# Chaining the score products and the value products of a sliding-window attention so that two head groups alternate on TensorE

## The chip, the cores and the metric

The kernel runs on one core of one Trainium2 chip. The metric is the device time of one execution in microseconds. Three runs of the kernel before gave 2683.91, 2685.73 and 2686.53 us; their median is 2685.73 us.

## What is computed

One decoder block over 2048 tokens of width 1024, in float32: an adaptive norm, one wide projection, two token mixers side by side (sliding-window attention with sinks, and a chunkwise mLSTM), their gated merge, and a SwiGLU feed-forward part. The change touches only the attention. Cut to that:

```python
# 8 query heads in 2 groups of 4, one key/value head of width 64 to each group
# blocks of 128 queries; each sees its own and the previous block of 128 keys
s = einsum('bnqhgd,bnkhd->bnhgqk', qb, kb)          # scores, 128 x 256 to a head
s = where(mask, s, -inf)
m = maximum(max(s), sink)
p = exp(s - m); p = p / (sum(p) + exp(sink - m))
o = einsum('bnhgqk,bnkhd->bnqhgd', p, vb)           # values with probabilities
```

## The kernel before

**Stages.** The sequence is worked in two superblocks of 1024 tokens. In each, the projection's big products (tiles `acc`, left operand `whi`/`wlo` or `big`, written as a high and a low part so that three float32r products make one of float32 accuracy) fill TensorE, and the attention and the mLSTM are woven between them as generators ("streams"). After both superblocks comes the feed-forward part, with no attention in it. The streams of superblock 0 that matter here run from 99 to 300 us of the profiled execution, those of superblock 1 from 774 to 977 us.

**One attention block** (`attention`, line 899) has 128 queries, n = 0 to 15. Two streams (`attention_stream`, line 980) take the even and the odd n. Its steps:

- Lines 915 to 931, twice (a half step each, `jj` = 0 and 1): two PSUM banks, one for each head group g, from a pool of four (`mix`). Twelve score products follow: two heads `u`, three products each (high with high, high with low, low with high), and for each of them g = 0 and g = 1. A product of g = 0 uses rows 0 to 63 of TensorE's array, one of g = 1 rows 64 to 127, because each head is 64 wide. ScalarE then copies the bank out (line 927) and VectorE merges the other half of the keys in (line 929).
- Lines 932 to 946: maximum, exponentials on ScalarE (line 942), sums, and a multiplication by the reciprocal on GpSimd (line 946).
- Lines 949 to 961: for each g, four transposes of the probabilities on TensorE (line 216), a copy on ScalarE (line 955, `pf`) and, for n > 0, a masked copy on VectorE (line 959, `pc`).
- Lines 962 to 965: four products of values with probabilities, `pf` of g = 0 and 1, then `pc` of g = 0 and 1 (two for n = 0). A product of g = 0 fills columns 0 to 63 of the array, one of g = 1 columns 64 to 127. Each shows as two matmul records in the trace.
- Lines 967 to 975: ScalarE casts the sum out (line 968) and issues DMAs for it and for the next block's operands (lines 970, 896, 975).

**What sets the order.** The generators fix the order in which instructions are traced. Before line 1576 each instruction is pinned to that order; after it a list scheduler orders each engine's instructions anew, by its own estimate of when operands are ready and buffers free. It keeps data dependencies and the few explicit order edges, nothing else, so products that are traced in turn need not stand in turn. `mm` (line 207) issues a matmul and returns nothing. [...]

In the profile all products of `mm` have line 211 and all transposes line 216: they are told apart by their tiles. `mix<-at` are scores, `mix<-tm,at` the products with values, `acc<-...` the projection.

## Time and profile before

| what | value |
|---|---|
| median of three runs | 2685.73 us |
| the profiled execution | 2687.54 us, of which the span is 2685.5 us |
| TensorE busy | 2629.6 us (98% of the span), 12382 matmul records |
| VectorE, ScalarE, GpSimd busy | 1988.3, 1298.8, 140.4 us |
| score products | 384, from 99.3 to 949.5 us |
| products with values | 62 (124 records), from 124.0 to 976.8 us |
| granted TensorE clock, mean | 0.993 |

How to read it: a row of the timeline gives the start, the time from the first start to the last end of the merged instructions, engine, line, operation, tiles, shapes and count; in brackets stand the idle time of that engine ahead of the row and what ended it. Matmuls overlap in the array, so what one costs is read from its start to the start of the next, not from its length.

### The profile page before, as it was taken

The numbers are of one execution on the slowest core, as the hardware profiler recorded it, in microseconds if no ns is written. First come the engines' busy times: TensorE is split into PE (matmuls) and PEld (weight loads), VectorE is DVE, ScalarE is ACT, GpSimd is POOL, SyncE is SP. The second block draws the span as 40 slices with busy tenths as digits, with TensorE's granted clock in tenths as the row PEclk, the third lists the DMA queues.
The fourth block names the chain that finished last, engine by engine and source line by source line (L and its number), as shares of the span: only waits on it lengthen the run. The fifth ranks groups of instructions, "written<-read, shape, count | busy, mean of one in ns | idle before, by whom it ended". The sixth has DMA issues, their size and how long they took to land.

```text
span 2685.5 us, 35800 instructions
## 1 busy us (share of the span) xinstructions
PE 2629.6 (98%) x12382; PEld 2146.8 (80%) x12382; DVE 1988.3 (74%) x3882; ACT 1298.8 (48%) x2525; POOL 140.4 (5%) x181
## 2 busy tenths in 40 slices
PE   7899999999998999999999999999999999999998
PEld 6777788888886778888877888888777888888886
DVE  7888887768696988876677777775677676666466
ACT  4656544545754654444654343335554333333444
POOL 0100001200101000110000000000000000000000
PEclk9999999999999999999999999999999999999999
DMA  7564456897575644678775555446675232334566
GB/s 252 173 231 144 148 175 185 263 345 246 191 245 160 210 141 151 194 239 321 227 243 176 181 180 180 134 143 219 214 247 188 98 114 97 108 99 148 189 204 219
DMA packets 353637, 511.89 MB, mean 191 GB/s; under 512 B 25120, under 2 KB 213660, under 8 KB 348208
## 3 DMA queue, kind: packets, MB, share of 16 engines
q1 hardware_dynamic: 335240, 493.82, 55.4%
q10 hardware_dynamic: 18216, 15.79, 2.0%
q8 instruction: 97, 1.59, 0.2%
q14 instruction: 84, 0.69, 0.1%
HBM read 357.12 MB, written 144.02 MB: 187 GB/s over the span
## 4 chain that ended last, share of the span: by engine, by line
PE 63%; DVE 3%; DMA 1%; ACT 1%; issue 0%; POOL 0%; SPq 0%; DVEq 0%; POOLq 0%; ACTq 0%
PE acc L211 42%; PE mix L211 20%; DVE hl L1608 1%; PE mix L216 1%; DMA raw<-as_d 1%; ACT hl L1607 1%; DMA raw<-ws_d 0%; DMA raw<-in_w_ffn_down_dram 0%; DVE big L1608 0%; DVE w L1918 0%; DVE big L1931 0%; DVE w L1954 0%; DVE w L1959 0%; ACT big L1653 0%; POOL rs L457 0%
## 5 line engine op out<-in xcount | busy, mean ns | idle before, releaser
L211 PE MATMUL acc<-big,hl 128*128 128x512 f32 x3936 | 933.9, 392 | 1.4 <-ACT hl L1607 0.7
L211 PEld LDWEIGHTS acc<-big,hl 128*128 128x128 f32 x3936 | 732.9, 188 | 164.8 <-issue 10.0
L1607 ACT CAST hl<-raw 128x512 fp32r<-128x512 f32 x732 | 440.7, 621 | 504.7 <-PE acc L211 238.7
L1608 DVE TENSOR_TENSOR hl<-raw,hl 128x512 fp32r<-128x512 f32 x732 | 497.5, 695 | 190.1 <-ACT hl L1607 187.8
L211 PE MATMUL acc<-whi,big 128*128 128x512 f32 (+1 forms) x1216 | 356.7, 374 | 7.9 <-ACT tx L89 3.8
L211 PE MATMUL mix<-big,hl 128*128 128x512 f32 x1056 | 263.0, 390 | 1.7 <-ACT hl L1607 1.0
L211 PEld LDWEIGHTS acc<-whi,big 128*128 128x128 f32 x1216 | 222.1, 191 | 50.9 <-ACT tx L89 4.3
L211 PE MATMUL acc<-hl,hl 128*128 128x512 f32 x1008 | 238.8, 395 | 5.8 <-DVE hl L1608 3.4
L211 PEld LDWEIGHTS mix<-big,hl 128*128 128x128 f32 x1056 | 197.7, 188 | 44.5 <-ACT hl L1607 1.9
L211 PEld LDWEIGHTS acc<-hl,hl 128*128 128x128 f32 x1008 | 188.0, 189 | 52.1 <-DVE hl L1608 8.4
L211 PE MATMUL acc<-wlo,big 128*128 128x512 f32 (+1 forms) x608 | 226.0, 374 | 3.0 <-DVE wlo L267 3.0
L211 PE MATMUL mix<-hl,hl 128*128 128x512 f32 x792 | 182.6, 391 | 1.1 <-DVE hl L1608 0.9
L211 PEld LDWEIGHTS mix<-hl,hl 128*128 128x128 f32 x792 | 147.9, 188 | 34.8 <-DVE hl L1608 3.0
L211 PE MATMUL acc<-big,whi 128*128 128x512 f32 x512 | 158.2, 393 | 0.0
L267 DVE TENSOR_TENSOR wlo<-raw,whi 128x1024 fp32r<-128x1024 f32 (+1 forms) x95 | 109.8, 1156 | 64.6 <-ACT whi L266 58.4
L266 ACT CAST whi<-raw 128x1024 fp32r<-128x1024 f32 (+1 forms) x95 | 93.7, 987 | 112.5 <-PE acc L211 102.5
L211 PEld LDWEIGHTS acc<-wlo,big 128*128 128x128 f32 x608 | 115.6, 190 | 24.0 <-DVE wlo L267 4.6
L457 POOL TENSOR_TENSOR rs<-ms,halves 128x1 f32<-128x1 f32 (+1 forms) x56 | 43.6, 791 | 1647.1 <-DVE ms L455 1637.5
L211 PE MATMUL mix<-hcT4h,hl 128*128 128x512 f32 x352 | 115.6, 389 | 0.7 <-ACT hl L1607 0.7
L211 PE MATMUL acc<-hcT2h,hl 128*128 128x512 f32 x352 | 115.5, 389 | 0.0
L211 PEld LDWEIGHTS acc<-big,whi 128*128 128x128 f32 x512 | 95.4, 188 | 19.6 <-DMA big<-y_d 0.4
L211 PE MATMUL acc<-big,wlo 128*128 128x512 f32 x256 | 97.6, 392 | 0.0
(350 smaller groups left out, 3537.2 us busy)
## 6 DMA issues: line engine op xcount, KB each, us to landing
raw<-in_w_in_dram SPq DMA_DIRECT2D x48, 1024.0 KB, 6.7
as_d<-w SPq DMA_DIRECT2D x154, 256.0 KB, 2.1
raw<-as_d SPq DMA_DIRECT2D x70, 512.0 KB, 3.9
raw<-in_w_ffn_gate_dram SPq DMA_DIRECT2D x22, 1024.0 KB, 5.5
raw<-in_w_ffn_up_dram SPq DMA_DIRECT2D x22, 1024.0 KB, 6.0
raw<-ws_d SPq DMA_DIRECT2D x40, 512.0 KB, 4.6
tx<-in_w_ada_dram SPq DMA_DIRECT2D x64, 256.0 KB, 3.7
g_d<-tx SPq DMA_DIRECT2D x64, 256.0 KB, 2.5
```

Source lines behind the costliest of these rows:

```text
L211: T.matmul(o, lhsT=lhsT, rhs=rhs, start=start, stop=stop, skip_group_check=resumed)
L216: T.transpose(o, i, ident[:k, :k])
L266: A.copy(hv, src)
L267: V.tensor_tensor(lv, src, hv.bitcast(F32), op=ALU.subtract)
L457: G.tensor_tensor(r[:, :n], ms[:, :n], nhalf[:, :n], op=ALU.pow)
L1607: A.copy(v(hi), src)
L1608: V.tensor_tensor(v(lo), src, v(hi).bitcast(F32), op=ALU.subtract)
```

## The change

`mm` now returns its instruction. `mm_chain` makes a product stand behind the one before it of the same chain, on TensorE's own queue, as an order edge without a wait for its result. The twelve score products of a half step make one chain, the products with values of one block another. Other instructions may still stand between two links.

```diff
-        T.matmul(o, lhsT=lhsT, rhs=rhs, start=start, stop=stop, skip_group_check=resumed)
+        return T.matmul(o, lhsT=lhsT, rhs=rhs, start=start, stop=stop, skip_group_check=resumed)
+
+    def mm_chain():
+        last = []
+
+        def one(o, lhsT, rhs, start, stop):
+            with ExitStack() as order:
+                if last:
+                    order.enter_context(tc.issue_after(last[0]))
+                last[:] = [mm(o, lhsT, rhs, start, stop).ins]
+        return one
...
+                paired = mm_chain()
                 for u in range(2):
                     j = 2 * jj + u
                     for lt, rt, st_, sp_ in ((qth, kth, True, False), (qth, ktl, False, False), (qtl, kth, False, True)):
                         for g in range(2):
                             pr = slice(g * 64, (g + 1) * 64)
-                            mm(banks[g, jj][:, u * 256 + k0:u * 256 + 256], lt[pr, j, :], rt[pr, ks], st_, sp_)
+                            paired(banks[g, jj][:, u * 256 + k0:u * 256 + 256], lt[pr, j, :], rt[pr, ks], st_, sp_)
...
             yps = mix_tile()
+            paired = mm_chain()
             for src_, u, st_, sp_ in ((pfs, int(first), True, first), (pcs, 1, False, True)):
                 for g, p_ in enumerate(src_):
-                    mm(yps[g * 64:(g + 1) * 64, :], vat[:, u, g * 64:(g + 1) * 64], p_.rearrange("p j q -> p (j q)"), st_, sp_)
+                    paired(yps[g * 64:(g + 1) * 64, :], vat[:, u, g * 64:(g + 1) * 64], p_.rearrange("p j q -> p (j q)"), st_, sp_)
```

The instructions are the same; the scheduler orders them differently on TensorE, VectorE, ScalarE and SyncE, within the two stretches of attention named above. From the last attention block to the end, every engine's order is what it was. Lines behind 211 stand 10 to 12 further down in the changed kernel (216 is 226 there, 942 is 953, 955 is 966, 968 is 980).

Three places follow. **TensorE, a half step at 197 us.** Bank `mix_2142` is that of g = 0, `mix_2143` that of g = 1; `acc` rows are the projection. Before:

```order
L211 MATMUL acc_1974<-wlo_2036,big_992 128x512
L211 MATMUL mix_2142<-at_2045 128x256 x6
L211 MATMUL acc_1974<-whi_2035,big_993 128x512
L211 MATMUL mix_2143<-at_2045 128x256 x6
L211 MATMUL acc_1971<-whi_2114,big_992 128x512
```

and now:

```order
L211 MATMUL acc_1971<-whi_2114,big_993 128x512
L211 MATMUL mix_2142<-at_2045 128x256
L211 MATMUL acc_1971<-whi_2114,big_992 128x512
L211 MATMUL mix_2143<-at_2045 128x256
L211 MATMUL mix_2142<-at_2045 128x256
L211 MATMUL mix_2143<-at_2045 128x256
L211 MATMUL mix_2142<-at_2045 128x256
```

The six of g = 0 and the six of g = 1 stood as two blocks with the projection between them. Now the first product of g = 0 stands alone, and behind one or more rows of the projection the other eleven follow in turn (the last seven are left out here).

**TensorE, the products with values of two blocks at 240 us.** Bank `mix_2348` is one block's, with `tm_2310` for g = 0 and `tm_2332`, `tm_2334` for g = 1; `mix_2360` is the other's, with `tm_2323`, `tm_2325` for g = 0 and `tm_2344`, `tm_2346` for g = 1. Before:

```order
L211 MATMUL mix_2348<-tm_2332,at_2045 64x512
L211 MATMUL mix_2348<-tm_2310,at_2045 64x512
L211 MATMUL mix_2360<-tm_2323,at_2047 64x512
L211 MATMUL mix_2360<-tm_2344,at_2047 64x512
L211 MATMUL mix_2348<-tm_2334,at_2045 64x512
L211 MATMUL mix_2360<-tm_2325,at_2047 64x512
L211 MATMUL acc_2741<-big_1576,hl_2719 128x512
```

and now, behind the first two and seven rows of the projection:

```order
L211 MATMUL mix_2360<-tm_2323,at_2047 64x512
L211 MATMUL mix_2360<-tm_2344,at_2047 64x512
L211 MATMUL mix_2360<-tm_2325,at_2047 64x512
L211 MATMUL acc_2741<-big_992,hl_2801 128x512
L211 MATMUL mix_2348<-tm_2334,at_2045 64x512
L211 MATMUL acc_2741<-big_993,hl_2801 128x512
L211 MATMUL mix_2360<-tm_2346,at_2047 64x512
```

Six products in one piece, g = 1, 0, 0, 1, 1, 0, became pieces of two, three and one; the eighth stood alone before and still does.

**ScalarE at 123 to 129 us**, where block n = 0 ends and block n = 1 has its exponentials. `tm_1154` and `tm_1155` are the scores of n = 1, `mix_1271` is the bank of the products with values of n = 0. Before:

```order
L955 COPY tm_1262<-mix_1257 128x512
L942 ACTIVATE tm_1154,sums_1152<-tm_1154,nmx_1151 128x128
L938 ACTIVATE es_1153<-es_1153 128x8
L942 ACTIVATE tm_1154,sums_1152<-tm_1154,nmx_1151 128x128 x3
L942 ACTIVATE tm_1155,sums_1152<-tm_1155,nmx_1151 128x128 x4
L968 CAST tm_1274<-mix_1271 128x512
L896 DMA at_1278<-at_d_192 128x1792
L970 DMA y_d_222<-tm_1274 128x4x128
```

and now:

```order
L966 COPY tm_1262<-mix_1257 128x512
L980 CAST tm_1274<-mix_1271 128x512
L906 DMA at_1278<-at_d_192 128x1792
L982 DMA y_d_222<-tm_1274 128x4x128
L949 ACTIVATE es_1153<-es_1153 128x8
L953 ACTIVATE tm_1154,sums_1152<-tm_1154,nmx_1151 128x128 x4
L953 ACTIVATE tm_1155,sums_1152<-tm_1155,nmx_1151 128x128 x4
```

The exponentials of n = 1 stood ahead of the cast of n = 0's result; now they stand behind the cast and behind two DMA issues. TensorE's order at this place is unchanged: products with values of n = 0 from `tm_1244`, four rows of the projection, from `tm_1262`, then the transposes of `tm_1154`.

## The prediction

> **What bounds the kernel now.** I read the page first, then the busy time by stretches, then TensorE's timeline around the attention, then all engines where TensorE waits.

> ```profile
> span 2685.5 us, 35800 instructions
> PE acc L211 42%; PE mix L211 20%; DVE hl L1608 1%; PE mix L216 1%; DMA raw<-as_d 1%; ACT hl L1607 1%; DMA raw<-ws_d 0%; DMA raw<-in_w_ffn_down_dram 0%; DVE big L1608 0%; DVE w L1918 0%; DVE big L1931 0%; DVE w L1954 0%; DVE w L1959 0%; ACT big L1653 0%; POOL rs L457 0%
> ...
> core 0: us, PE busy (x) PEld busy (x) DVE busy (x) ACT busy (x) POOL busy (x), PEclk, DMA share, GB/s
> 98.00:146.00 48.00, 42.84 (x266) 33.48 (x265) 40.53 (x96) 32.41 (x84) 4.12 (x4) 0.96 0.59 189
> 146.00:250.00 104.00, 103.89 (x508) 77.00 (x507) 83.54 (x210) 64.13 (x167) 9.60 (x9) 1.00 0.56 186
> 860.00:985.00 125.00, 125.00 (x620) 93.91 (x619) 112.51 (x233) 80.16 (x193) 9.54 (x8) 1.00 0.57 185
> ```

> TensorE's products lead the chain that ended last. In most of the attention's time TensorE never stops (103.89 of 104.00 us, 125.00 of 125.00), so there the time is the sum of what its instructions take, in their order. In the first 48 us of attention it stands still for 5.2 us: there the time is set by waits. I cost the change in these two currencies, against the profiled execution of 2687.5 us (2.0 us beside the span), which lies 1.8 us above the median of the runs.

> **First term: how the products are arranged on TensorE.** Prices come from the order before.

> ```profile
> 195.84 0.62 PE L211 MATMUL acc<-whi,big 128*128 128x512 f32 x2
> 196.29 0.39 PE L211 MATMUL acc<-wlo,big 128*128 128x512 f32 x1
> 196.61 0.97 PE L211 MATMUL mix<-at 64*128 64x256 f32 x6
> 197.51 0.49 PE L211 MATMUL acc<-whi,big 128*128 128x512 f32 x1
> ...
> 198.84 0.50 PE L211 MATMUL acc<-whi,big 128*128 128x512 f32 x1
> 199.18 0.40 PE L211 MATMUL acc<-wlo,big 128*128 128x512 f32 x1
> ...
> 250.31 0.98 PE L211 MATMUL mix<-at 64*128 64x256 f32 x12
> 251.22 0.96 PE L211 MATMUL acc<-big,hl 128*128 128x512 f32 x3
> ...
> 255.99 1.69 PE L211 MATMUL mix<-at 64*128 64x256 f32 x24
> 257.61 0.97 PE L211 MATMUL acc<-big,hl 128*128 128x512 f32 x3
> ...
> 135.20 0.38 PE L211 MATMUL mix<-at 64*128 64x256 f32 x1
> 135.51 1.07 PE L211 MATMUL mix<-tm,at 128*64 128x512 f32 x2
> ...
> 785.99 1.32 PE L211 MATMUL mix<-at 64*128 64x256 f32 x12
> 787.25 0.39 PE L211 MATMUL acc<-wlo,big 128*128 128x264 f32 x1
> ```

> A projection product steps on in 0.225 us (195.84 to 196.29 for two). Ahead of a piece of scores it takes 0.32, the first behind one 0.34 (198.84 to 199.18): going into and out of the half-array form costs 0.095 + 0.115 = 0.21. Six scores of one group take 0.90 (196.61 to 197.51), twelve of both groups 0.91, twenty-four 1.62: two groups in turn cost what one does, 0.118 for each further pair. With the 0.21, a piece of six is 1.11, of twelve 1.12, of twenty-four 1.83, and one score alone 0.31 + 0.21 = 0.52. Twelve at 785.99 stand as six and six that adjoin, as the order before has it: 1.26, partly side by side.

> A half step in two blocks of six costs 2.22. As the order of the change has it, one alone and eleven in turn, it costs 0.52 + 1.12 = 1.64: 0.58 saved, not 1.10, since the first product still goes alone. In superblock 0 five half steps change so: -2.9. But one that alternated already is cut into 1 and 11 (+0.52), and three that stood as 24 and 12 (2.95) become 12, 1, 12 and 11 (3.88, +0.93).

> The products with values:

> ```profile
> 177.16 1.08 PE L211 MATMUL mix<-tm,at 128*64 128x512 f32 x4
> 178.17 0.50 PE L211 MATMUL acc<-wlo,big 128*128 128x512 f32 x1
> ...
> 233.15 1.07 PE L211 MATMUL mix<-tm,at 128*64 128x512 f32 x2
> 234.15 0.96 PE L211 MATMUL acc<-big,hl 128*128 128x512 f32 x3
> ...
> 239.81 2.80 PE L211 MATMUL mix<-tm,at 128*64 128x512 f32 x12
> 242.54 1.20 PE L211 MATMUL acc<-big,hl 128*128 128x512 f32 x4
> ```

> One (two records) takes 1.00, two of both groups 1.01, six 2.73, so 0.86 for each further pair; with 0.21 for the change of form a piece of one is 1.21, of two 1.22, of three 2.08, of five or six 2.94. From 233.15 on the pieces 1, 6, 1 (5.36) become 1, 2, 3, 1, 1 (6.93): +1.57. At the next two blocks 1, 6, 1 become 1, 5, 1, 1 (6.57): +1.21. The chain of one block holds its own products in turn, but it parts those of the two streams, which before had met in one piece. Superblock 0 comes to -2.9 + 0.52 + 0.93 + 1.57 + 1.21 = +1.3. Superblock 1 at the same prices has four half steps that gain (-0.2 where only the second half is cut, -0.6, and -0.6 for the two that adjoin, 2.94 against 0.52 + 1.83: some -1.3), one cut (+0.5) and one place of values (+0.5): -0.3. **Arrangement: +1.0 us**; bounds -0.5 and +2, since a score next to its neighbours' pieces may overlap more or less than the rows above.

> [...]

> **Second term: a chain on ScalarE.**

> ```profile
> 120.22 1.11 PE L216 MATMUL mix<-ident,tm 128*128 128x128 f32 x4 [3.10 <-POOL tm L946]
> ...
> 123.56 0.58 ACT L955 COPY tm<-mix 128x512 f32<-128x512 f32 x1
> ...
> 124.03 0.42 ACT L942 ACTIVATE tm<-tm,nmx 128x128 f32<-128x128 f32 x1
> ...
> 125.73 1.07 PE L211 MATMUL mix<-tm,at 128*64 128x512 f32 x2
> ...
> 126.90 1.04 POOL L946 TENSOR_TENSOR tm<-tm,sums 128x512 f32<-128x512 f32 x1 [5.74 <-PE mix L211]
> ...
> 127.22 0.57 ACT L968 CAST tm<-mix 128x512 fp32r<-128x512 f32 x1
> ...
> 127.82 0.40 ACTq L970 DMA_DIRECT2D y_d<-tm  x1
> ...
> 127.99 0.66 PE L216 MATMUL mix<-ident,tm 128*128 128x128 f32 x4 [1.19 <-POOL tm L946]
> ```

> TensorE waits at 127.99 for GpSimd's normalised scores of n = 1, and those come from the exponentials that ScalarE began at 124.03, right behind the copy of 123.56. In the change's order these exponentials stand behind the cast of n = 0's result (127.22, which waits for the product of 125.73), the issue of its DMA (to 128.22) and one small exponential (0.2): they start near 128.4, **4.4 us later**, and nothing on TensorE stands in between to fill the time, since transposes of n = 1 are next in its queue. Behind them, the sums, the multiplication and the transposes shift whole. What TensorE gained earlier is in the first term, and it carries through if n = 0's exponentials start earlier too, which ScalarE's order allows (one copy of n = 1 now stands behind them). Bounds: 0, if the cast is early enough to be hidden, and 5.

> **Third term: the granted clock.**

> ```profile
> 116.50:119.70 3.20, 0.61 (x6) 0.38 (x4) 1.96 (x11) 3.20 (x16) 0.58 (x1) 1.00 0.01 1
> 119.70:123.10 3.40, 2.88 (x14) 2.89 (x15) 3.40 (x7) 2.75 (x5) 1.46 (x2) 0.51 0.00 0
> ```

> Behind a stretch with 0.61 us of products in 3.20 the clock was 0.51 for 3.4 us: up to 1.7 us of work lost. The wait of n = 1 grows from 1.19 to some 5.6 us, enough for one more such stretch, while the earlier wait of 3.10 may shrink. I take **+0.8**, half of it; bounds -1.7 and +1.7. [...]

> **Fourth term: two later shifts on ScalarE.**

> ```profile
> 177.24 0.60 ACT L773 COPY tx<-acc 128x512 f32<-128x512 f32 x1
> ...
> 180.63 0.59 ACT L968 CAST tm<-mix 128x512 fp32r<-128x512 f32 x1 [2.79 <-PE mix L211]
> ...
> 779.23 2.18 ACT L535 CAST big<-big 128x512 fp32r<-128x512 f32 x4 [2.23 <-DMA big<-big]
> ...
> 782.21 0.59 PE L211 MATMUL acc<-whi,big 128*128 128x264 f32 x1 [2.52 <-ACT tx L819]
> ```

> The copy of 177.24 frees a bank of the projection; in the new order it stands behind the cast of 180.63, which itself waits for the last product with values. Cast and copy are 1.2 us, of which TensorE's transposes cover some: +0.9 (bounds 0 and 1.2). In superblock 1 the four casts of 779.23 now stand ahead of one more copy that frees a bank; TensorE already waits 2.52 us there, and a third of the casts' 2.18 more is +0.8 (bounds 0 and 2.2).

> **Sum:** 1.0 + 4.4 + 0.8 + 0.9 + 0.8 = +7.9, so 2695.4 for the profiled execution and **2693.5 us** for the median.

> **Rivals.**

> - *The waits are covered.* DMAs and streams drift so that ScalarE's cast is done before the exponentials could start anyway. Then only the arrangement stays: +1.0, 2686.7 us. For it: elsewhere the attention hides everything (125.00 busy of 125.00). Against it: the wait at 127.99 is there already, before anything is put ahead of it.
> - *Faster: alternation pays and the cuts are free.* Single products go where TensorE would have waited, so the gains of 4.2 (2.9 + 1.3) stay whole, and the softmax of n = 0 comes early enough that the wait of 3.10 falls below what drops the clock: 1.3 of wait and 1.7 of clock. That is -7.2 on 2685.7, 2678.5 us. It decides only if the ScalarE term is below 2 us. Against it: the cut pieces stand among projection products that never wait.
> - *Banks run short.* A half step's first product now takes its bank of four and holds it until its partner's is free, so transposes and sums that want banks queue behind. If each of the nine places adds one copy of 0.6 us, that is +5.4 more: 2699 us.
> - *It does not do what it says.* The first product still runs alone in nine places and in the values the streams part; this is in the first term already, priced, and has no time of its own.

> **How the numbers follow.** Forecast (2689 to 2698) 0.55, covered waits 0.20, short banks 0.17, faster 0.08. A difference of 0.2% (5.4 us) is what a measurement here can tell from none: slower means above 2691.1, faster below 2680.4. The forecast's own range puts some 0.05 below 2691.1. So slower 0.50 + 0.17 = 0.67, faster 0.07, the same 0.26. The range of eight in ten reaches from just under the covered case, 2685, to 2701, past the short banks.

> **What would show it.** In the new profile: a wait for GpSimd at the transposes of n = 1 of about 5 us where 1.19 stood, with ScalarE idle behind the copy of line 966 until the cast of line 980; single scores of about 0.5 us at nine places or more; products with values in more and shorter pieces behind 233 us; a second half-clock stretch near 130 us; from 300 to 770 us and behind 980 us the same times, shifted. Wrong would be: the wait unchanged or gone, single scores that cost 0.12, or the feed-forward part itself moved by over 2 us.

## The result, and the profile after

The changed kernel took 2693.95 us (median of six runs, 2692.05 to 2697.12) beside 2685.40 us for the kernel before: a ratio of **1.0035**, with a 95% interval of 1.0022 to 1.0047. It is slower by 8.55 us. Its profiled execution took 2697.12 us, the longest of the six, and 9.58 us more than that of before. On its page TensorE's products still lead the chain that ended last, with 40 and 19% of the span where before they had 42 and 20%. To see where the time went, the attention of superblock 0 and what follows is cut into stretches that hold the same work in both kernels: each cut is the start of a TensorE instruction ahead of which both have carried out the same set. Busy time by stretches, before:

```profile
core 0: us, PE busy (x) PEld busy (x) DVE busy (x) ACT busy (x) POOL busy (x), PEclk, DMA share, GB/s
99.34:121.12 21.78, 18.68 (x122) 15.74 (x123) 19.32 (x52) 14.62 (x40) 2.00 (x2) 0.97 0.55 180
121.12:131.70 10.58, 8.87 (x44) 5.61 (x43) 7.39 (x17) 8.59 (x27) 2.12 (x3) 0.90 0.34 87
131.70:145.14 13.44, 13.44 (x93) 10.82 (x92) 11.65 (x21) 7.55 (x16) 0.00 (x0) 1.00 0.80 268
145.14:183.54 38.40, 38.29 (x180) 26.59 (x179) 28.73 (x96) 22.55 (x68) 5.43 (x5) 1.00 0.55 172
183.54:302.15 118.61, 118.61 (x593) 90.38 (x592) 98.28 (x213) 77.31 (x190) 9.10 (x8) 1.00 0.53 176
302.15:733.30 431.15, 430.64 (x2076) 360.43 (x2074) 332.08 (x693) 224.25 (x398) 41.03 (x43) 1.00 0.69 230
733.30:998.98 265.68, 253.49 (x1320) 194.92 (x1321) 224.69 (x537) 154.44 (x376) 20.29 (x17) 0.97 0.58 189
```

and the same stretches after:

```profile
95.06:116.84 21.78, 17.40 (x123) 14.12 (x122) 18.99 (x50) 15.04 (x41) 2.08 (x2) 0.96 0.53 178
116.84:132.96 16.12, 11.53 (x43) 7.73 (x43) 8.57 (x20) 9.52 (x28) 2.08 (x2) 0.74 0.33 91
132.96:146.33 13.37, 12.91 (x93) 10.09 (x92) 9.25 (x17) 6.87 (x15) 0.00 (x0) 1.00 0.70 242
146.33:185.75 39.42, 38.44 (x181) 26.85 (x180) 31.13 (x101) 23.44 (x70) 5.53 (x5) 1.00 0.57 174
185.75:307.80 122.05, 122.05 (x592) 90.11 (x590) 101.74 (x214) 76.25 (x186) 8.34 (x8) 1.00 0.48 160
307.80:740.90 433.10, 431.07 (x2076) 360.44 (x2076) 330.58 (x688) 225.49 (x400) 40.69 (x43) 1.00 0.69 230
740.90:1008.89 267.99, 253.74 (x1320) 193.98 (x1321) 221.13 (x536) 153.61 (x374) 18.67 (x17) 0.97 0.58 187
```

The first number behind the times is the length, the next TensorE's busy time; their difference is its waiting. Set side by side:

| stretch (of before) | length, before and after | difference | of it TensorE busy | waiting |
|---|---|---|---|---|
| 99 to 121 us | 21.78, 21.78 | 0.00 | -1.28 | +1.28 |
| 121 to 132 us | 10.58, 16.12 | +5.54 | +2.66 | +2.88 |
| 132 to 145 us | 13.44, 13.37 | -0.07 | -0.53 | +0.46 |
| 145 to 184 us | 38.40, 39.42 | +1.02 | +0.15 | +0.87 |
| 184 to 302 us | 118.61, 122.05 | +3.44 | +3.44 | 0 |

Superblock 0 costs 9.93 us more, most of it in two places: 5.54 where n = 0 ends, half of it waiting and half TensorE's own work at a lower clock (0.74 for 0.90), and 3.44 where TensorE never waits, all of it the arrangement of its products. Another 1.02, nearly all waiting, lies between 145 and 184 us. From 302 to 733 us the order is the same and TensorE's busy time nearly too (430.64 and 431.07); the stretch is 1.95 us longer all the same. Superblock 1 is 2.31 us longer. Against this stands a start that ran 4.28 us shorter (99.34 and 95.06), in the same order: drift of single executions, taken up below.

TensorE's waits in superblock 0, from its timeline (in brackets the idle time and what ended it):

```profile
114.44 0.70 PE L226 MATMUL mix<-ident,tm 128*128 128x128 f32 x4 [2.67 <-POOL tm L957]
116.84 1.12 PE L226 MATMUL mix<-ident,big 128*128 128x128 f32 x4 [1.71 <-DVE tm L940]
...
128.44 1.02 PE L226 MATMUL mix<-ident,tm 128*128 128x128 f32 x4 [4.58 <-POOL tm L957]
...
182.89 0.50 PE L211 MATMUL acc<-whi,big 128*128 128x512 f32 x1 [0.80 <-ACT tx L783]
```

The wait for GpSimd at the transposes of n = 1 is 4.58 us where 1.19 stood; that of n = 0 shrank from 3.10 to 2.67, and 1.71 for a copy of VectorE is new behind it (line 940, which reads the next block's scores out of a bank; these transposes read `big`, so what they need of that copy is the bank); 0.80 is the forecast wait for the copy of line 783. ScalarE's timeline shows why the first is so long:

```profile
120.61 0.59 ACT L966 COPY tm<-mix 128x512 f32<-128x512 f32 x1 [1.16 <-PE mix L226]
123.89 0.59 ACT L980 CAST tm<-mix 128x512 fp32r<-128x512 f32 x1 [2.69 <-PE mix L211]
124.03 0.37 ACTq L906 DMA_DIRECT2D at<-at_d  x1
...
125.07 0.39 ACT L953 ACTIVATE tm<-tm,nmx 128x128 f32<-128x128 f32 x1
```

From the copy to the first exponential of n = 1 it is 4.46 us (120.61 to 125.07), where before it was 0.47 (123.56 to 124.03): in between ScalarE stands idle for 2.69 us, for the last product with values of n = 0. Its rows stand in the order that the scheduler set: copy, cast, DMA issue, exponentials.

The clock at the same place, in pieces of 3.4 us, the length that its own steps have (in windows of 0.1 us it is at half from 119.74 to 123.15 us in before, here from 114.92 to 121.75 and from 128.58 to 131.99 us: 3.41, 6.83 and 3.41 us):

```profile
111.50:114.90 3.40, 0.73 (x7) 0.45 (x5) 1.36 (x9) 3.40 (x18) 1.11 (x2) 1.00 0.15 56
114.90:118.30 3.40, 1.69 (x9) 1.46 (x8) 3.36 (x6) 2.66 (x7) 0.97 (x1) 0.50 0.00 0
118.30:121.70 3.40, 3.40 (x13) 2.17 (x12) 2.63 (x7) 1.74 (x3) 0.00 (x0) 0.50 0.00 0
...
125.10:128.50 3.40, 0.06 (x1) 0.07 (x2) 1.93 (x7) 3.14 (x17) 1.04 (x1) 1.00 0.82 246
128.50:131.90 3.40, 3.40 (x16) 3.12 (x16) 0.90 (x3) 2.13 (x4) 1.04 (x1) 0.51 0.56 171
```

Three pieces at half clock, two in a row and one behind the long wait, where before there was one. Each follows a piece with few products: 0.73, 1.69 and 0.06 us of 3.40. Last, the pieces that TensorE's products stand in: a half step at 199 us and the products with values behind 241 us:

```profile
199.34 0.39 PE L211 MATMUL acc<-whi,big 128*128 128x512 f32 x1
199.66 0.38 PE L211 MATMUL mix<-at 64*128 64x256 f32 x1
199.97 0.49 PE L211 MATMUL acc<-whi,big 128*128 128x512 f32 x1
200.40 0.98 PE L211 MATMUL mix<-at 64*128 64x256 f32 x11
201.30 0.50 PE L211 MATMUL acc<-wlo,big 128*128 128x512 f32 x1
201.64 0.63 PE L211 MATMUL acc<-whi,big 128*128 128x512 f32 x2
...
241.56 1.07 PE L211 MATMUL mix<-tm,at 128*64 128x512 f32 x2
...
251.28 1.93 PE L211 MATMUL mix<-tm,at 128*64 128x512 f32 x6
```

From 199.34 to 201.64 is 2.30; without three projection products at 0.225 the half step in 1 and 11 costs 1.63, and the prediction had 1.64. The products with values that had stood as 1, 6 and 1 are 1, 2, 3, 1, 1 now (two records to a product).

### The profile page after: what moved, and what is told of

It is laid out like the page before. It is cut to its first block, busy times and chain, and to the rows that moved or that the text cites. A ratio compares the mean times of both kernels' runs of the same rounds, so it can differ in the third digit from the quotient of the medians.

```text
span 2695.4 us, 35804 instructions
## 1 busy us (share of the span) xinstructions
PE 2631.5 (98%) x12382; PEld 2143.4 (80%) x12382; DVE 1987.2 (74%) x3882; ACT 1299.0 (48%) x2525; POOL 137.8 (5%) x181
## 4 chain that ended last, share of the span: by engine, by line
PE 60%; DMA 3%; DVE 3%; ACT 1%; issue 0%; SPq 0%; POOL 0%; DVEq 0%; POOLq 0%; ACTq 0%
PE acc L211 40%; PE mix L211 19%; DVE hl L1620 1%; PE mix L226 1%; DMA big<-y_d 1%; DMA raw<-as_d 1%; DMA raw<-in_w_branch_attn_dram 1%; ACT hl L1619 1%; DMA raw<-in_w_ffn_down_dram 1%; DMA raw<-ws_d 0%; DVE big L1620 0%; DVE w L1930 0%; DVE big L1943 0%; DVE w L1971 0%; DVE w L1966 0%
## 5 line engine op out<-in xcount | busy, mean ns | idle before, releaser
L211 PE MATMUL acc<-big,hl 128*128 128x512 f32 x3936 | 936.3, 392 | 1.4 <-ACT hl L1619 0.7
L211 PEld LDWEIGHTS acc<-big,hl 128*128 128x128 f32 x3936 | 732.7, 188 | 167.7 <-issue 11.7
L211 PE MATMUL acc<-whi,big 128*128 128x512 f32 (+1 forms) x1216 | 359.1, 375 | 8.3 <-ACT tx L89 3.8
L211 PE MATMUL mix<-big,hl 128*128 128x512 f32 x1056 | 263.1, 390 | 1.7 <-ACT hl L1619 1.0
L211 PEld LDWEIGHTS acc<-whi,big 128*128 128x128 f32 x1216 | 223.7, 192 | 51.3 <-ACT tx L89 4.3
L211 PE MATMUL acc<-hl,hl 128*128 128x512 f32 x1008 | 237.1, 393 | 5.9 <-DVE hl L1620 3.3
L211 PEld LDWEIGHTS mix<-big,hl 128*128 128x128 f32 x1056 | 197.8, 188 | 44.6 <-DVE hl L1620 1.9
L211 PE MATMUL acc<-wlo,big 128*128 128x512 f32 (+1 forms) x608 | 227.1, 375 | 3.7 <-DVE wlo L277 3.7
L211 PEld LDWEIGHTS acc<-hl,hl 128*128 128x128 f32 x1008 | 187.0, 188 | 51.5 <-DVE hl L1620 8.8
L211 PE MATMUL mix<-hl,hl 128*128 128x512 f32 x792 | 182.8, 391 | 1.2 <-DVE ms L465 0.5
L211 PEld LDWEIGHTS mix<-hl,hl 128*128 128x128 f32 x792 | 147.9, 188 | 35.3 <-DVE hl L1620 2.9
L211 PE MATMUL acc<-big,whi 128*128 128x512 f32 x512 | 158.2, 393 | 0.6 <-DMA big<-y_d 0.6
L211 PEld LDWEIGHTS acc<-wlo,big 128*128 128x128 f32 x608 | 116.5, 192 | 23.6 <-DVE wlo L277 5.3
L211 PE MATMUL mix<-hcT4h,hl 128*128 128x512 f32 x352 | 115.6, 389 | 0.7 <-ACT hl L1619 0.7
L211 PE MATMUL acc<-hcT2h,hl 128*128 128x512 f32 x352 | 115.5, 389 | 0.0
L211 PEld LDWEIGHTS acc<-big,whi 128*128 128x128 f32 x512 | 95.4, 188 | 20.3 <-DMA big<-y_d 1.1
L211 PE MATMUL acc<-big,wlo 128*128 128x512 f32 x256 | 97.8, 393 | 0.0
```

The source lines that it names most:

```text
L211: return T.matmul(o, lhsT=lhsT, rhs=rhs, start=start, stop=stop, skip_group_check=resumed)
```

## The experiments

The theory: ScalarE's late exponentials of n = 1 and the half clock behind the wait make the larger part, the order of TensorE's pieces the rest. The rivals: the pieces alone, the banks that a lone first product holds, and superblock 1. The ratio is to the kernel before, with its 95% interval; it differs from the quotient of the medians by up to 0.0007.

| kernel | median us | ratio |
|---|---|---|
| chain of values alone | 2685.13 | 1.0001 (0.9990 to 1.0013) |
| score chain for n = 1 alone | 2689.42 | 1.0019 (1.0008 to 1.0029) |
| score chains from n = 8 on | 2684.59 | 1.0002 (0.9990 to 1.0015) |
| score chains below n = 8 | 2694.04 | 1.0028 (1.0017 to 1.0040) |
| changed, cast behind the exponentials | 2693.15 | 1.0027 (1.0015 to 1.0038) |
| changed, cast and DMA issue behind them | 2688.64 | 1.0013 (1.0003 to 1.0024) |
| score chains for n = 2 to 7 | 2691.92 | 1.0020 (1.0008 to 1.0032) |
| changed, waits filled | 2695.28 | 1.0035 (1.0021 to 1.0050) |
| before, waits filled | 2688.14 | 1.0013 (1.0000 to 1.0025) |
| changed, no lone first product | 2696.57 | 1.0041 (1.0026 to 1.0056) |
| the same, cast and DMA issue behind | 2697.07 | 1.0042 (1.0027 to 1.0057) |

The median of the kernel before, run beside them, was 2683.97, 2684.63 and 2686.75 us in the three sets.

**The chain of values alone.**

```diff
-                            paired(banks[g, jj][:, u * 256 + k0:u * 256 + 256], lt[pr, j, :], rt[pr, ks], st_, sp_)
+                            mm(banks[g, jj][:, u * 256 + k0:u * 256 + 256], lt[pr, j, :], rt[pr, ks], st_, sp_)
```

> The chain on the score products is taken out, the one on the products with values is kept. My theory, from the orders of the two kernels: the value chain moves no instruction on any engine, so the time is that of before, 2685 us, ratio 0.999 to 1.001, with the wait of 1.19 us at the transposes of n = 1 and the value pieces 1, 6, 1 behind 233 us. The rival is what my prediction said of the cut pieces (the chain of one block parts the products of the two streams): then 1.57 + 1.21 = 2.8 us more than before, 2688 us.

It is the kernel before: 1.0001, and the order of every engine is that of before. (With the score chain alone, which was not timed by itself, the order of every engine is that of the changed kernel.) So the cut pieces of values come with the score chain, by way of the scheduler, which orders every engine anew. The rival falls by the order; the interval alone would not exclude its 2.8 us.

It also shows how far two executions of one order drift apart. Its stretches from 302 and from 733 us of before:

```profile
299.56:732.77 433.21, 430.60 (x2076) 360.48 (x2074) 332.55 (x693) 224.66 (x399) 40.64 (x43) 1.00 0.68 229
732.77:1000.27 267.50, 254.82 (x1320) 196.62 (x1321) 224.65 (x537) 153.63 (x374) 20.26 (x17) 0.96 0.58 188
```

They are 2.06 and 1.82 us longer than those of before with the very same order (1.95 and 2.31 in the changed kernel). The first holds a wait at its end for the low parts of weights, and so it does in the changed kernel:

```profile
732.77 0.59 PE L211 MATMUL acc<-wlo,big 128*128 128x264 f32 x1 [2.52 <-DVE wlo L277]
```

```profile
740.90 0.39 PE L211 MATMUL acc<-wlo,big 128*128 128x264 f32 x1 [1.84 <-DVE wlo L277]
```

In before it was 0.48 us. The second has 1.33 us more of busy time, with the clock at 0.96 for 0.97. Elsewhere this execution is shorter: its first score product starts at 96.06 us for 99.34, and what follows both stretches takes 1682.3 us for 1686.5 in before and in the changed kernel. So the 1.95 and 2.31 us of the changed kernel's profile need no cause in its order, nor do the 4.28 us at its start.

**Score chains in one superblock.** Two kernels, with `n >= 8` and `n < 8`:

```diff
-                paired = mm_chain()
+                paired = mm_chain() if n >= 8 else mm
```

> Only the score products of superblock 1 (n from 8 on) are chained, besides the chains of values; superblock 0 stands as before. My prediction's terms for superblock 1 are -0.3 for the arrangement and +0.8 for the casts ahead of a copy on ScalarE: +0.5 us. The two traces set beside each other give +2.7 us between 750 and 976 us. Theory: +1 to +3 us (ratio 1.0004 to 1.0011). Rival: the loss of superblock 1 in the changed kernel came from transfers that stood elsewhere against the clock and the waits, as one DMA wait of 0.96 us at 780 us hints; alone it would then be within 0.5 us of before.

> Only the score products of superblock 0 (n below 8) are chained, besides the chains of values. The orders of superblock 0 are then those of the changed kernel on every engine, superblock 1 stands nearly as before (15 pieces of scores for 13, worth +0.9 us by the prices of my prediction). Theory: superblock 0 carries the whole loss; its terms were 1.3 + 4.4 + 0.8 + 0.9 = 7.4, with the 0.9 it is +8 us (ratio 1.0025 to 1.0035). Rival: the two superblocks share it, as the traces of before and after say (9.9 and 2.7 us, of which some is drift): then +5 to +6 us (ratio 1.002).

Superblock 1 alone measures 1.0002, superblock 0 alone 1.0028: about 0.5 and 7.5 us. The whole loss is that of superblock 0 as far as the intervals tell; the rival that shares it is not excluded at their edges. The stretches of the second kernel, cut as above, are 15.62 and 122.05 us for the 16.12 and 122.05 of the changed kernel.

**The score chain for n = 1 alone.**

```diff
-                paired = mm_chain()
+                paired = mm_chain() if n == 1 else mm
```

> Only the twelve score products of block n = 1 (two half steps) are chained, besides the chains of values. On ScalarE the cast of n = 0's result then stands ahead of the exponentials of n = 1, as in the changed kernel, while the score pieces are 32 and the single ones 1, against 30 and 1 before and 35 and 9 in the changed kernel. My theory: the ScalarE chain and the clock behind it carry most of the loss. The wait for GpSimd at the transposes of n = 1 is 4 to 5 us, a longer half-clock stretch than before's 3.4 us stands between 110 and 135 us, and the time is 5 to 7 us above before (ratio 1.002 to 1.0026). Rival: the cut pieces on TensorE carry the loss: then at most +1 us (ratio below 1.0005), and the wait is filled by work that moves into it.

```profile
119.50:135.17 15.67, 11.09 (x42) 7.79 (x42) 8.36 (x20) 9.82 (x28) 2.56 (x3) 0.76 0.34 94
```

Two half steps chained are enough for the whole of the first place: 15.67 us where before has 10.58, with the clock at 0.76, and 1.0019, or 5.1 us, by the runs. Its profiled execution, 2696.06 us, is the longest of its twelve, so the trace shows the mechanism better than the size. From 184 to 302 us this kernel takes 120.78 us, 2.17 more than before, 0.86 of it waiting; its pieces there are neither those of before nor those of the changed kernel. So not all of the 5.1 us need come from the first place, but the wait of 4.58 us, the clock and the time are what the theory said.

**The cast behind the exponentials, then the DMA issue too.** The first kernel adds an order edge to the changed one, the second puts the load of the next block's operands under it as well:

```diff
-                    A.activation(sc[g][:, j, :], sc[g][:, j, :], AF.Exp, bias=nm_[:, hd:hd + 1], accum_out=sums[:, hd:hd + 1])
+                    exps[n] = A.activation(sc[g][:, j, :], sc[g][:, j, :], AF.Exp, bias=nm_[:, hd:hd + 1], accum_out=sums[:, hd:hd + 1]).ins
...
-            A.copy(yh, yps)
+            with ExitStack() as order:
+                if n == 0:
+                    order.enter_context(tc.issue_after(exps[n + 1]))
+                A.copy(yh, yps)
...
-                later = load_at(n + 2, nc.scalar)
+                with ExitStack() as order:
+                    if n == 0:
+                        order.enter_context(tc.issue_after(exps[n + 1]))
+                    later = load_at(n + 2, nc.scalar)
```

> The changed kernel with one more order edge: the cast of n = 0's result stands behind the last exponential of n = 1 on ScalarE, as it did before the change. In superblock 0 TensorE's order is that of the changed kernel but for seven rows near 148 us. In superblock 1 the scheduler's order differs more: 19 pieces of scores and 19 of values for the changed kernel's 15 and 15, by the prices of my prediction 4.1 us more. Theory (ScalarE chain): the wait for GpSimd at the transposes of n = 1 falls from 4.58 to about 1.2 us, one half-clock stretch less stands between 110 and 135 us, and the stretch from 98 to 300 us is 4 to 6 us shorter than in the changed kernel. With the 4.1 us of superblock 1 the whole time is about that of the changed kernel, +6 to +10 us. Rival: the gain is given back at the next bank that ScalarE's late cast frees; then the stretch from 98 to 300 us is within 2 us of the changed kernel's, and the whole +11 to +14 us.

The first missed: the wait was 3.93 us, not 1.2, and the stretch from 98 to 300 us is 1.2 us shorter than in the changed kernel (211.55 for 212.74), not 4 to 6. That the whole, some 7.2 us over before, lies within the +6 to +10 expected is luck. ScalarE's timeline in it shows what took the cast's place:

```profile
123.79 0.58 ACT L966 COPY tm<-mix 128x512 f32<-128x512 f32 x1 [1.17 <-PE mix L226]
126.58 0.37 ACTq L906 DMA_DIRECT2D at<-at_d  x1
127.00 0.40 ACT L953 ACTIVATE tm<-tm,nmx 128x128 f32<-128x128 f32 x1 [2.63 <-PE mix L211]
```

The issue of the load of the next operands stands between the copy and the exponentials and waits, as the cast did, for the last product with values. Hence the second kernel, in which only that issue's place differs:

> As the kernel whose cast of n = 0's result stands behind the exponentials of n = 1, and the issue of the DMA for the next block's operands (line 906) behind them too. There that issue still stood ahead of the exponentials and ran at 126.58 us, behind the last product of values of n = 0, with ScalarE idle for 2.63 us ahead of the exponentials and TensorE for 3.93 us at the transposes of n = 1. Every engine but ScalarE has the very same order in both. Theory (any instruction of ScalarE that waits for that product holds the exponentials, cast or DMA issue): now the exponentials start right behind the copy, the wait at the transposes of n = 1 falls to 1 to 2 us, one half-clock stretch of 3.4 us less stands at the start, the stretch between the anchors at 121 and 131.7 us of before takes 0 to +2 us more than before where it took 4.4, and the whole is 2 to 4 us below that kernel: +3.5 to +6 us over before (ratio 1.0013 to 1.0022). Rival: the exponentials wait for something else (the maximum, the scores' bank); then nothing changes.

```profile
119.28 0.59 ACT L966 COPY tm<-mix 128x512 f32<-128x512 f32 x1 [1.16 <-PE mix L226]
119.77 0.40 ACT L953 ACTIVATE tm<-tm,nmx 128x128 f32<-128x128 f32 x1
```

The exponentials follow the copy at once. The stretch from 121 us of before, first with the cast moved alone and then with both:

```profile
120.02:135.00 14.98, 11.05 (x42) 7.57 (x43) 8.69 (x21) 9.51 (x28) 2.08 (x2) 0.76 0.30 98
```

```profile
115.59:126.75 11.16, 9.47 (x43) 6.09 (x43) 8.00 (x19) 9.42 (x29) 2.56 (x3) 0.85 0.33 101
```

14.98 us become 11.16, and before has 10.58: the 5.54 us are gone but for 0.58. Of the 3.82 won, 2.24 is waiting and 1.58 the clock. The medians of the two kernels are 4.5 us apart (each has its own set of runs of before; by the ratios it is 1.0027 and 1.0013, some 3.8 us). The two intervals overlap, so it is the trace that carries this: the first place is ScalarE's queue, and it had two holders, either of which is enough. In the stretch from 145 us of before 1.1 us of this come back in the trace, since TensorE, now earlier, waits 1.14 us for a DMA at 142.37 us (0.19 in the changed kernel). What the kernel still loses, 0.13% or 3.5 us, is about what the pieces of superblock 0 cost: its stretch from 184 to 302 us is 122.06 us long, as in the changed kernel. Superblock 1 has more pieces than there; the 4.1 us that the first expectation put on them would lift the sum above the interval's end of 6.4 us, so that price is not borne out.

**Score chains for n = 2 to 7.**

```diff
-                paired = mm_chain()
+                paired = mm_chain() if 2 <= n < 8 else mm
```

> Score chains for n = 2 to 7 only, besides the chains of values. The exponentials of n = 1 stay ahead of the cast of n = 0's result, as before; 20 pieces of scores and 20 of values in superblock 0 for 17 and 17, 5 single scores. By the prices of my prediction the arrangement costs +2.2 us in superblock 0 and +0.8 in superblock 1. Theory: no wait is added, so +2 to +4 us (ratio 1.0008 to 1.0015). Rival (banks run short): each of the four more single products holds a bank and puts off a copy by 0.6 us, so +5 to +7 us (ratio 1.002 to 1.0026), with new waits of TensorE for copies of ScalarE or VectorE between 150 and 300 us.

1.0020, some 5.4 us: the rival's size, though the theory's 2 to 4 lie in the interval. But not its mechanism: from 150 to 300 us TensorE waits 0.8 us for ScalarE's copy of line 783, as in the changed kernel, and for no other copy. What the theory had too low is shown by the stretch from 184 us on, all of it busy but for 0.36 us:

```profile
187.00:309.92 122.92, 122.56 (x592) 90.02 (x590) 102.21 (x214) 76.31 (x186) 8.33 (x8) 1.00 0.47 159
```

4.31 us more than before, and 3.44 in the changed kernel. By the terms of the prediction this stretch has +3.65 (its pieces there are those of the changed kernel). The +2.2 of superblock 0 was smaller only because it took off 1.1 us for pieces near 140 us, a stretch that is not shorter here (13.67 us for 13.44). The theory of no added wait failed too: at 131 us TensorE waits 1.82 us for a copy of VectorE (line 970), and the clock is at half a second time behind it (131.08 to 134.49 us); the stretch from 121 us takes 12.83 us for 10.58. This profiled execution too, 2696.42 us, is the longest of its twelve. The losses of the two parts, 5.1 and 5.4 us, add up to more than the 7.5 of superblock 0; their intervals, some 3 us to each side, allow it.

**Waits filled with small products.** Ten products of the identity with itself, overwritten by the transposes, in the changed kernel and in that of before:

```diff
                 pt = mix_tile()
+                if n < 2 and g == 0:
+                    for r in range(10):
+                        T.matmul(pt[:, :P], lhsT=ident, rhs=ident, start=True, stop=True)
```

> The changed kernel, with ten added products of 128x128 (the identity with itself, into the bank that the transposes then overwrite) ahead of the first transposes of n = 0 and of n = 1, where TensorE waits for GpSimd 2.67 and 4.58 us. Ten take some 2.7 us at full clock by the transposes of the same shape (1.11 for four), so they fit into the waits. Theory: the half-clock stretches of 6.8 us at 114.9 and 3.4 us at 128.6 come from TensorE standing idle; with the products they go or shrink by a half, the wait is still there but filled, and the time is 1.5 to 4 us below the changed kernel's: 2690 to 2692.5 us, ratio to before 1.0017 to 1.0027. Rival: the stretches do not hang on these waits; then they stay, and the products, which also move a few instructions around them, make it 0 to 4 us slower than the changed kernel.

> The kernel before, with the ten added products of 128x128 ahead of the first transposes of n = 0 and of n = 1, where it waits for GpSimd 3.10 and 1.19 us. Ten took 3.88 us and 2.50 us in the changed kernel with the same products (2.5 at full clock). Theory: the one half-clock stretch of the start (3.4 us, up to 1.7 us of work) goes, nothing else gets later; -0.5 to -2 us, ratio 0.9993 to 0.9998, too little to be told from no change. Rival: as in the changed kernel with these products, the filled wait turns into a new one for a bank behind it: 0 to +3 us.

In the changed kernel the half clock shrank to one piece of 3.4 us (116.44 to 119.85 us), as the theory had it. The time didn't follow, 1.0035, though its interval leaves room for some of the gain. By the count of its instructions, the added ones left out, TensorE was some 4.4 us ahead of the changed kernel at 146 us, and some 1.5 us ahead 3 us later. What happened there, by the timelines of TensorE and of ScalarE:

```profile
148.58 0.50 PE L211 MATMUL acc<-whi,big 128*128 128x512 f32 x1 [2.67 <-ACT tx L808]
```

```profile
146.07 2.18 ACT L545 CAST big<-big 128x512 fp32r<-128x512 f32 x4 [3.96 <-DMA big<-big]
148.16 0.37 ACT L808 COPY tx<-acc 128x264 f32<-128x264 f32 x1
```

Four casts on ScalarE wait 3.96 us for a DMA, and the copy that frees TensorE's bank stands behind them: TensorE, here the earlier one, waits for that DMA. This wait of 2.67 us is nearly all of what was lost there. But over superblock 0 as a whole the trace keeps a gain: from the five projection products ahead of the first scores (93.81 us, and 90.64 in the changed kernel) to the cut at 738.60 us (740.90) it takes 644.79 us for 650.26. Why the medians show nothing of these 5.5 us stays open; two executions of one order differed by some 2 to 4 us in a stretch, as shown above. In the kernel before, the half-clock piece at 120 us went (the clock is 1.00 from 95 to 155 us), and the time was 1.0013 of before: the rival's side, but its interval reaches 1.0000.

**No lone first product.** A small product at the head of each chain, into the other group's bank, makes the first score wait for both banks; the second kernel adds the two order edges on ScalarE from above:

```diff
                 paired = mm_chain()
+                paired(banks[1, jj][:, :16], qth[:, 0, :], kth[:, k0:k0 + 16], True, True)
```

> The changed kernel with one small product (128 rows, 16 columns, whole array, overwritten by the scores) at the head of each score chain, into the bank of g = 1, so that no score product goes before that bank is free. By its order no single score is left and all half steps but one alternate as twelve; the cast of n = 0's result still stands ahead of the exponentials of n = 1. By the prices of my prediction its pieces cost 3.5 us less than before in superblock 0 and 0.5 less in superblock 1; the 32 added products cost some 0.06 to 0.21 us each, 2 to 6.7 us. Theory: the ScalarE term stays (+5), the pieces' gain in the stretches that wait is lost: +4 to +8 us over before, ratio 1.0015 to 1.003; a half step of twelve shows 1.1 us from its first score to the next projection product. Rival (holding the banks was the cost): without single scores the time falls below +3 us.

> As the kernel with the small product at the head of each score chain, and with the cast of n = 0's result and the issue of the next DMA behind the exponentials of n = 1 on ScalarE; TensorE's order is the same but for eight rows. Both suspected costs are gone: the ScalarE chain and the single scores. Theory: 3 to 5 us below the kernel without this edge, -1 to +3 us against before (ratio 0.9996 to 1.0011), the difference lying between 121 and 132 us. Rival: the loss is spread over waits elsewhere; then it stays above +4 us.

Both missed, 1.0041 and 1.0042. The pieces are as wanted: two half steps in turn and the added products stand in one row at 208.32 us of the second kernel, 1.1 us each. Alternation as the change meant it, in all half steps but one and with the added products, does not make the kernel faster. The ScalarE edges move nothing here: already without them no transposes wait 4 us for GpSimd at the start, and other waits bound it, of the kind that the theory did not count. TensorE's waits of the second kernel from 95 to 300 us (total, times, longest):

```profile
PE mix L226 <- DVE tm L941: 3.4, 2, 2.0
PE mix L226 <- POOL tm L958: 1.8, 1, 1.8
PE mix L211 <- ACT tm L967: 1.7, 1, 1.7
```

The first three waits, ahead of transposes at 112, 115 and 118 us, leave the clock at half for three pieces of 3.4 us (112.28 to 122.52 us). In superblock 1, between 730 and 1010 us, TensorE's waits add up to 18.4 us, where before has 12.6 and the execution of the chain of values alone 15.2; the longest is 5.93 us for GpSimd at 845.93 us, where before has 2.53. This makes the rival (the loss is spread over waits elsewhere) the better reading, but which of these waits the added products caused was not tried. The profiled executions of both, 2690.8 and 2692.5 us, are 5 us below their medians, so the rest of the loss can't be read from them.

## Why the prediction was right, point by point

- **The sum** was right: +7.9 us forecast (2693.5), +8.55 measured (2693.95). Its terms were not all of the right size.
- **ScalarE chain, +4.4.** The mechanism is shown by the kernel with both order edges. The size was somewhat high: the exponentials came 4.0 us later behind the copy (4.46 for 0.47), the wait grew by 3.39 (1.19 to 4.58; in the second execution of before's order it is 0.32), the waiting of the whole stretch by 2.88. The step counted the DMA issues as time behind the cast; the issue of line 906 is a holder of its own.
- **Granted clock, +0.8.** Too small, and outside its bounds of 1.7: the same work took 2.66 us more of TensorE's time there. The step that failed is to count half of one more half-clock stretch: there are two more, one behind the wait of n = 1, as forecast, and one ahead of it. The one ahead needs no new wait of 1.71 us: the kernel with the chains below n = 8, whose wait for line 940 is 0.21 us, has it too, and the one with the chain for n = 1 alone has it behind a single wait of 3.11 us, up to 118.30 us:

```profile
113.45:116.85 3.40, 1.74 (x17) 1.34 (x16) 1.26 (x10) 2.73 (x15) 0.00 (x0) 1.00 0.21 71
116.85:120.25 3.40, 1.87 (x8) 1.48 (x9) 2.96 (x7) 3.40 (x11) 2.38 (x2) 0.50 0.00 0
```

  Here the wait lies across two pieces, and the clock is at half up to 123.69 us; in before a wait of 3.10 us fell mostly into one piece and cost one. What decides where the pieces lie stays open, so this part of the 2.66 us may be luck of the execution. A piece need not be empty for the clock to be at half behind it: in the changed kernel those with 0.73 and 1.69 us of products were followed by half clock too.
- **Both together** were 5.2 forecast and 5.54 measured: one error balanced the other, which is luck.
- **Arrangement, +1.0.** The prices held: the stretch without waits, at 184 to 302 us, gives +3.65 by them (-0.58 + 0.52 + 0.93 + 1.57 + 1.21) and +3.44 in the trace. Two steps failed. One is the count of "five half steps": near 135 us two of them stood as 6, 1, 11 and 6 and became 1, 1, 11 and 11, which by the prices saves 0.58 for both and not for each. The other is "What TensorE gained earlier is in the first term, and it carries through". In the stretches of 99 to 121 and 132 to 145 us TensorE's work became 1.28 and 0.53 us shorter, by prices 1.16 and 0.58, and the waiting 1.28 and 0.46 us longer: next to waits a gain of TensorE can be worth nothing, and it must not simply be set against losses elsewhere. Part of it can stay: with waits for line 940 of 0.21 and 0.71 us, the first stretch took 21.02 and 20.78 us in the kernels with the chains below n = 8 and with both order edges, for 21.78. In the changed kernel's trace the term is +3.4 for superblock 0, not +1.3.
- **The chain of values parts the streams' products**: wrong. The pieces are cut as forecast, but by the score chain.
- **Later shifts.** The copy of line 783: 0.9 forecast, 0.87 more waiting between 145 and 184 us. The casts in superblock 1: that superblock alone gives 1.0002, which fits the +0.5 forecast for it and can't tell it from nothing.
- **The rivals.** Covered waits did not happen. Banks running short: nine lone products, but of the copies that were to add 0.6 us each TensorE's waits from 150 to 300 us show none beside line 783's. Ahead of that there is one wait for a bank, the 1.71 us for line 940 at 116.84 us; it is 0.21 to 1.34 us in the kernels that have the same order there, and neither before nor the kernels with chains for n = 1 alone and for n = 2 to 7 have it. The rival is right in kind at that one place. Freed of lone products, with a small product added to each chain, the change does what it says, and is no faster.

## What to carry to other kernels

Cut the trace into stretches of equal work and split each difference into busy time and waiting before adding gains and losses: a saving on an engine that waits at the end of the same stretch can become waiting (1.28 us did between 99 and 121 us), a loss in a stretch without waits is paid in full (3.44 us between 184 and 302 us). An order edge in a scheduled program reorders every engine, so read what it moves on the engines that it doesn't name: two half steps chained cost 5 us here, most of it by way of ScalarE's queue. When something is moved out of the way in a queue, look for the next instruction behind it with the same wait, DMA issues too (with that of line 906 still ahead, the wait of 4.58 us was 3.93).

## What the runs showed of the hardware

```profile
195.53 0.62 PE L211 MATMUL acc<-whi,big 128*128 128x512 f32 x2
195.99 0.17 PE L211 MATMUL mix<-at 128*128 128x16 f32 x1
196.02 0.48 PE L211 MATMUL acc<-whi,big 128*128 128x512 f32 x1
```

Two projection products and the added one take 0.49 us from the first start to the next projection product, where two alone step on by 0.45: 0.04 us, below the 0.06 that the expectation had as the lower end.
